# Second mixer of a two-layer trunk: seven block products for half of the values, with weight sums formed earlier and kept in HBM

## The chip, the core and the metric

The kernel runs on one core of a Trainium2 chip. The metric is the device time of one execution in microseconds, as a median over several runs. The engines that matter are TensorE (PE, matmuls), VectorE (DVE), ScalarE (ACT) and GpSimd (POOL). DMA transfers are issued from the queue of SyncE (SP) and, for a few, from POOL's or ACT's queue.

## The reference, cut to what matters

The program is a trunk of two layers over 256 tokens of width 1024. In each layer come an FFN, a mixer and an FFN, each behind an RMS norm and with its result added to the stream. The change bears on the second layer's mixer and on the two FFNs ahead of it (the second FFN of layer 0 and the first of layer 1).

```
def swiglu(x, w_gate, w_up, w_down):
    return (jax.nn.silu(x @ w_gate) * (x @ w_up)) @ w_down
...
def c_mixer(x, w_in, w_out):
    q, k, v = jnp.split(x @ w_in, 3, axis=-1)
    o = moba_attention(to_heads(q, C_HEADS, C_HEAD_DIM),
                       to_heads(k, C_HEADS, C_HEAD_DIM),
                       to_heads(v, C_HEADS, C_HEAD_DIM))
    return from_heads(o) @ w_out
```

With 256 tokens and blocks of 256, the attention of this mixer is plain causal attention with 16 heads of 64. `w_in` is 1024 x 3072: 1024 columns of queries, of keys and of values. The values' first half is the product of the 256 x 1024 normed activations with 512 columns of `w_in`.

## The kernel before, in words

**Matmuls.** Every large product is done in three matmuls (`mm3`, L354 to L356): each operand is cut into a high part (fp32r) and the remainder, and high x high, high x low and low x high are summed in PSUM. An activation of width 1024 lies as 8 tiles of 128 rows, transposed: `xT["h"]` and `xT["l"]` (high part and remainder), with the gain of the norm in them; the norm's factor for a token (`norm["col"]`, `norm["row"]`) is applied after the product.

**Weights.** All weights lie in HBM as chunks of 128 x 2048, in the order in which the program uses them (`weight_chunks`, `_layout`). `Stream` loads a chunk into one of three raw buffers (`raw`, SP's queue), splits it on ACT (`whi`, L231) and DVE (`wlo`, L238) into one of four buffers for split weights, and frees this buffer after the matmuls. A unit is the chunk that one `take` hands out. The split of a unit, in two pieces of 1024 columns most times, is written into the program where an earlier unit is freed (`pump`). Units that come first in a stage keep part of their columns in another place of the buffer (`reset`), and then their pieces are 384, 384 and 1280 wide. A `summed` chunk gets its remainder from a DMA on POOL's queue that adds to what ACT wrote.

**The stages.** The stages are ffn (phase 0), the first mixer (1), ffn (2), ffn (3), the second mixer (4, `c_mixer`) and ffn (5). An FFN takes 22 units for gate and up and 12 for the down projection. In the last FFN, eight of the down projection's blocks are already done by seven products in place of eight. Their weight sums are formed during phases 2 and 3: `begin_sums` loads a chunk (`blocks`), DVE forms sums (L635 to L637), and SP stores them to HBM, at the positions that `AHEAD` lists. The pool for these tiles is the FFN's own.

**The next stage's activations.** `Next` belongs to the stage that follows. During the down projection of an FFN, `Next.pair` adds a finished pair of tiles to the stream, writes high part and remainder (L393 the remainder), and `squares` gathers the sum of squares (L403, L404).

**The second mixer.** Its units come in this order: q0, k0, the values' first half (two units of 4 x 512 columns), q1, k1, q2, k2, the values' second half, q3, k3, and the output projection. Each of the q and k units holds 256 columns, so four heads. `first_tiles` does q0 and k0: it starts with the k tiles that are done, and between them the mean of squares goes to PE (`sums`), POOL takes the root (`rstd`, L362), ACT spreads it over a tile (L473) and PE transposes that (L475, in `spread`). Then come the copies of q (L979 on ACT, L984 on DVE) and of k (L962 on DVE, L998 on ACT, L1000 and L1002 on POOL), four tiles one after another. `token_block` then does half of the values with the activations as the stationary operand: 2 token tiles x 8 tiles of the inner width x 3 matmuls of 512 columns, into two PSUM banks, and `put_v` scales them, writes the high part (L1169 on ACT) and the remainder (L1170 on DVE).

**The heads.** Attention work is slipped between the units. `step()` is called at fixed points of the program, and `Slots` says at which of them a head's scores, its transposition or a weighted sum is written. For one head, `scores` has PE do the product, DVE subtracts the maximum (L1025 adds the mask to one corner, L1040 does the rest in two parts), ACT takes the exponent (L1043) with the sum, DVE the reciprocal (L1046), and POOL scales the probabilities by it (L1050, in two parts of 128 and 256 columns). `turn` has PE transpose the three blocks of a head's probabilities (L1059), and splits them into `pth` and `ptl`. `weighted` multiplies two heads' probabilities with the values. The first four heads have their scores at steps 5 to 8, and their transpositions at steps 9, 9, 11 and 11.

**PSUM.** All eight banks come from one ring of buffers. Which bank an instruction writes, and so whose last reader it must wait for, follows from the order in which they are asked for.

## Time and profile before

| | us |
|---|---|
| median of 3 runs | 924.44 |
| lowest and highest | 923.64 and 924.46 |
| the profiled execution | 924.17 |
| its span in the profile | 922.4 |
| second mixer in it | about 634.4 to 744 |

A row of a timeline has the start in the span, the busy time, the engine and the line, output and inputs, the tile's shape, and how many such instructions follow one another. What stands in brackets is idle time before it and what ended that. PE's records are for pipelined matmuls, so that starts, not busy times, are to be compared. A row of a group has its count, the busy time in all with the mean in ns, and the idle time ahead of it.

### The profile page before, as it was taken

Reading aid. Unit: us, or ns where it says so; the run is one execution under the profiler, and the core shown is the slowest. Engines: PE = TensorE matmul, PEld = TensorE weight load, DVE = VectorE, ACT = ScalarE, POOL = GpSimd, SP = SyncE. Lnnn points to the kernel's source line nnn. Section 1 sums busy time; section 2 is a strip of 40 time slices with the busy share of each in tenths; the row PEclk is TensorE's granted clock in tenths of the full one; section 3 lists DMA queues with packets and bytes.
Section 4 is the critical chain, followed back from the end, with each engine's and each line's share of the span. In section 5 each row is a group of like instructions: output and inputs, shape, how many; then the busy total and the mean of one; then the engine's idle time right before and its main releaser. Section 6 shows DMA issues by size and latency. Waiting matters only on the chain.

```text
span 922.4 us, 18258 instructions
## 1 busy us (share of the span) xinstructions
PE 915.0 (99%) x7583; PEld 896.5 (97%) x7583; DVE 689.8 (75%) x1058; ACT 528.4 (57%) x808; POOL 80.8 (9%) x117
## 2 busy tenths in 40 slices
PE   9999999999999999999999999999999999999997
PEld 9999999999999999999999999999999999999886
DVE  7976556587888867655677666667778799978897
ACT  7754444468667545444564444455776777555574
POOL 0000000033310000000000000001565100000002
PEclk9999999999999999999999999999999999999999
DMA  9765554665256677766556878865533466855681
GB/s 325 272 228 183 180 195 174 228 226 181 93 183 230 220 281 266 296 238 218 187 209 236 305 272 313 318 216 192 184 137 137 119 230 225 277 191 206 223 310 60
DMA packets 33985, 202.15 MB, mean 219 GB/s; under 512 B 3904, under 2 KB 6208, under 8 KB 12528
## 3 DMA queue, kind: packets, MB, share of 16 engines
q1 hardware_dynamic: 32400, 197.79, 59.8%
q0 software_dynamic: 496, 1.77, 0.9%
q10 hardware_dynamic: 1008, 1.44, 0.5%
q8 instruction: 59, 0.97, 0.4%
q14 instruction: 22, 0.18, 0.1%
HBM read 188.14 MB, written 12.85 MB: 218 GB/s over the span
## 4 chain that ended last, share of the span: by engine, by line
PE 93%; issue 4%; DMA 2%; POOL 0%; DVE 0%; ACT 0%; POOLq 0%; DVEq 0%
PE bank L354 30%; PE bank L355 30%; PE bank L356 30%; DMA raw<-in_weights 1%; PE bank L1059 1%; DMA x<-blocks 1%; PE bank L601 1%; DMA xTl<-away 0%; POOL xTl L803 0%; DVE wlo L238 0%; PE bank L604 0%; PE bank L1021 0%; PE bank L1023 0%; PE bank L1022 0%; PE bank L1208 0%
## 5 line engine op out<-in xcount | busy, mean ns | idle before, releaser
L231 ACT ACTIVATE whi<-raw 128x1024 fp32r<-128x1024 f32 (+5 forms) x349 | 331.6, 994 | 280.4 <-issue 154.6
L238 DVE TENSOR_TENSOR wlo<-raw,whi 128x1024 fp32r<-128x1024 f32 (+5 forms) x349 | 390.6, 1149 | 78.8 <-ACT whi L231 77.8
L354 PE MATMUL bank<-xTh,whi 128*128 128x256 f32 x1600 | 442.7, 277 | 0.0
L356 PE MATMUL bank<-xTh,wlo 128*128 128x256 f32 x1600 | 441.8, 276 | 0.0
L355 PE MATMUL bank<-xTl,whi 128*128 128x256 f32 x1600 | 441.8, 276 | 0.0
L355 PEld LDWEIGHTS bank<-xTl,whi 128*128 128x128 f32 x1600 | 300.4, 188 | 0.0
L354 PEld LDWEIGHTS bank<-xTh,whi 128*128 128x128 f32 x1600 | 300.4, 188 | 0.0
L356 PEld LDWEIGHTS bank<-xTh,wlo 128*128 128x128 f32 x1600 | 300.4, 188 | 0.0
L356 PE MATMUL bank<-hTh,wlo 128*128 128x256 f32 x528 | 145.7, 276 | 0.0
L354 PE MATMUL bank<-hTh,whi 128*128 128x256 f32 x528 | 145.7, 276 | 0.0
L355 PE MATMUL bank<-hTl,whi 128*128 128x256 f32 x528 | 145.7, 276 | 0.0
L355 PEld LDWEIGHTS bank<-hTl,whi 128*128 128x128 f32 x528 | 99.1, 188 | 0.0
L354 PEld LDWEIGHTS bank<-hTh,whi 128*128 128x128 f32 x528 | 99.1, 188 | 0.0
L356 PEld LDWEIGHTS bank<-hTh,wlo 128*128 128x128 f32 x528 | 99.1, 188 | 0.0
L687 DVE TENSOR_TENSOR hm<-gs,bank 128x512 f32<-128x512 f32 x44 | 29.9, 683 | 45.4 <-PE bank L356 44.4
L954 POOL MEMSET k<- 64x256 f32 x12 | 3.2, 307 | 565.2 <-ACT whi L231 378.9
L684 DVE TENSOR_TENSOR gs<-bank,row 128x512 f32<-128x512 f32 x44 | 30.1, 686 | 21.3 <-PE bank L356 21.1
L354 PE MATMUL bank<-mixh,whi 128*128 128x256 f32 x128 | 35.7, 279 | 0.0
L356 PE MATMUL bank<-mixh,wlo 128*128 128x256 f32 x128 | 35.4, 277 | 0.0
L355 PE MATMUL bank<-mixl,whi 128*128 128x256 f32 x128 | 35.4, 276 | 0.0
L1050 POOL TENSOR_SCALAR pr<-pr,rl 128x128 f32<-128x128 f32 (+1 forms) x36 | 31.9, 899 | 29.5 <-DVE rl L1046 20.5
L359 ACT ACTIVATE hTh<-hm 128x512 fp32r<-128x512 f32 x44 | 27.1, 619 | 8.8 <-DVE hm L687 8.0
(231 smaller groups left out, 994.1 us busy)
## 6 DMA issues: line engine op xcount, KB each, us to landing
raw<-in_weights SPq DMA_DIRECT2D x139, 1024.0 KB, 5.0
raw<-in_weights SPq DMA_DIRECT2D x12, 768.0 KB, 4.8
blocks<-in_weights SPq DMA_DIRECT2D x9, 1024.0 KB, 10.0
blocks<-blocks SPq DMA_DIRECT2D x9, 1024.0 KB, 8.7
raw<-blocks SPq DMA_DIRECT2D x7, 1024.0 KB, 4.8
raw<-in_weights SPq DMA_DIRECT2D x6, 512.0 KB, 6.6
raw<-in_weights SPq DMA_DIRECT2D x7, 256.0 KB, 5.7
blocks<-block SPq DMA_DIRECT2D x5, 256.0 KB, 8.9
```

Of the source, the lines that this page charges most:

```text
L231: done = nc.scalar.activation(hi, r, AF.Copy)
L238: self.made[u] = done, nc.vector.tensor_sub(lo, r, hi.bitcast(F32))
L354: nc.tensor.matmul(p, sh, mh, start=start, stop=False)
L355: nc.tensor.matmul(p, sh, ml, start=False, stop=False)
L356: return nc.tensor.matmul(p, sl, mh, start=False, stop=stop)
L359: return nc.scalar.activation(hi, src, AF.Copy), nc.vector.tensor_sub(lo, src, hi.bitcast(F32))
L601: nc.tensor.matmul(o, w[0][i][:, cs], xT[m][:, k], start=k == 0 and m == "h" and j % 2 == 0, stop=False)
L684: nc.vector.tensor_mul(g, both(pg), twice(norm["row"]))
L687: nc.vector.tensor_mul(hm, g, both(pu))
L954: nc.gpsimd.memset(pair[j][o, 1].bitcast(F32), 0.0)
L1050: share = engine.tensor_scalar(pr[:, cs], pr[:, cs], rl[:, b : b + 1], None, op0=ALU.mult)
L1059: nc.tensor.transpose(tp[:, i * 128 : (i + 1) * 128], pr[:, i * 128 : (i + 1) * 128], ident)
```

## The change

The values' first half, a product of 2 x 8 tiles of activations with 8 x 2 blocks of 256 columns, is now done by seven block products for each pair of tiles in place of eight. For a pair of inner tiles the activations are four blocks a11, a21, a12, a22 of 128 x 128 and the weights four blocks of 128 x 256. Each of the seven products is three matmuls of 256 columns. The products use the plain blocks, four formed sums of activations and four formed sums of weights.

- **The weights' sums** are formed in phase 2, at positions 5 and 12 of the gate and up units (`FORMED`): `begin_formed` loads one of the two chunks (kind "V"), forms four sums on DVE (new L686 to L689), splits them into high part and remainder on ACT and DVE, and stores these with SP in HBM (new L699), 512 KB each, eight in all.
- **Their way into the mixer.** A V chunk gives two units in place of one. Each takes 768 plain columns out of the raw chunk, split as before in one piece (new L234 and L241), and 1024 formed columns, which two DMAs on POOL's queue bring straight into `whi` and `wlo` (new L246). So the block takes four units, with 21 matmuls of 256 columns each.
- **The activations' sums** of the first six tiles are formed in phase 3's down projection by `Next.form` (new L430 to L434: four combinations and a sum on DVE, then a split of 128 x 512), into tiles of a new pool. Those of the last pair are formed in `first_tiles`, into parts of the mixer's own tiles.
- **The fold.** The seven products lie in four PSUM banks: 1 and 2 share one, 6 has its own, 5 and 7 share one, 3 and 4 share one. ACT copies product 1 out (new L1254), five sums on DVE (new L1259 to L1263) make the two token tiles' values, and `put_v` reads them from SBUF.
- **Other moves.** In this mixer the copies of q0 are written right after its tiles, ahead of the unit of k0. The tiles `pth` and `ptl` come from a pool that is opened after the fold. The pool of `begin_sums` is closed ahead of the down projection.

The diff, cut:

```diff
+FORMED = {(2, 5): 0, (2, 12): 1}
...
+                pieces = [(slice(0, 768), src[:, (step - 3) * 1024 : (step - 3) * 1024 + 768])]
...
+        if step > 2:
+            self.parts[u] = tuple([t[:, i * 256 : (i + 1) * 256] for i in range(7)] for t in (his, los))
+            for to, v in zip((his, los), self.sums[j][step - 3]):
+                nc.gpsimd.dma_start(to[:, 768:1792], v)
+            split(0, raw[:, :768])
...
+        def form(self, i, f, hi, lo):
+
+            a11, a21, a12, a22 = (x1(2 * i + k)[:, t * 128 : (t + 1) * 128] for k in range(2) for t in range(NT))
+            g0, g1 = (self.gain(2 * i + k) for k in range(2))
+            m, s1, s2, s4 = (f[:, j] for j in range(4))
+            nc.vector.tensor_scalar(m, a22, g1, None, op0=ALU.mult)
+            for to, a, g, b, op in ((s1, a21, g0, m, ALU.add), (s2, a11, g0, s1, ALU.subtract),
+                                    (s4, a12, g1, s2, ALU.add)):
+                nc.vector.scalar_tensor_tensor(to, a, g, b, op0=ALU.mult, op1=op)
+            nc.vector.tensor_add(m, m, s2)
+            split(hi, lo, f)
...
+    def begin_formed(gp, i):
...
+            nc.sync.dma_start(t, st.weights[j].rearrange("(p c) -> p c", p=128))
+        yield
...
+        nc.vector.tensor_sub(b11, b12, b11)
+        nc.vector.tensor_sub(b12, b22, b12)
+        nc.vector.tensor_sub(b22, b11, b22)
+        nc.vector.tensor_add(b21, b21, b22)
...
+            split(hi, lo, f)
+            yield
+            with tc.issue_after(st.last.ins):
+                for to, v in zip(st.sums[j][k], (hi, lo)):
+                    nc.sync.dma_start(to, v.bitcast(F32))
+            yield
...
+                        if phase == 3 and c < 3:
+                            nxt.form(c, f, *(s[:, c] for s in nxt.forms))
...
+    def token_sevens(mix, v, p1, step):
...
+        pb = [bank() for _ in range(4)]
+        at = {1: (0, 0), 2: (0, 1), 6: (1, 0), 5: (2, 0), 7: (2, 1), 3: (3, 0), 4: (3, 1)}
...
+            for n, x, q in ((1, plain(0, 0), 0), (2, plain(0, 1), 1), (6, formed(2), 5), (5, formed(1), 3),
+                            (7, formed(0), 6), (3, formed(3), 2), (4, plain(1, 1), 4)):
+                mm3(p[n], *x, w[0][q], w[1][q], i == 0 and at[n][1] == 0, i == KD // 2 - 1 and n in (2, 6, 7, 4))
+            step()
+            st.free()
+        nc.scalar.activation(p1, p[1], AF.Copy)
...
+            nc.vector.tensor_add(u[:, 0], p1, p[6])
+            nc.vector.tensor_add(cv[:, 0], p1, p[2])
+            nc.vector.tensor_add(u[:, 1:], both(pb[2]), twice(u[:, 0]))
+            nc.vector.tensor_add(cv[:, 1:3], u[:, 1:], both(pb[3]))
+            nc.vector.tensor_add(cv[:, 3], u[:, 2], p[5])
+            for t in range(NT):
+                put_v(v, t, cv[:, 2 * t : 2 * t + 2].rearrange("p h c -> p (h c)"))
```

How the order of instructions changes is shown at three places. The first is DVE at the end of the values' block, before. `wlo` is the remainder of a weight piece, `pr` the probabilities of a head, `nm` its maximum, `rl` the reciprocal, `vtl` the remainder of the values.

```order
L1040 ISA pr,nm<-bank,mask,score 128x128
L1040 ISA nm 128x1
L1040 ISA pr,nm<-bank,mask,score 128x256
L1040 ISA nm 128x1
L238 TENSOR_TENSOR wlo<-raw,whi 128x1024
L1046 RECIPROCAL rl<-l 128x2
L238 TENSOR_TENSOR wlo<-raw,whi 128x1024
L1170 SCALAR_TENSOR_TENSOR vtl<-bank,rstd,vth 128x512
L984 TENSOR_TENSOR q<-bank,q 64x256 x2
L1025 TENSOR_TENSOR added<-bank,mask 128x128
```

The same place on DVE now, from the third head's maximum on; `u` and `cv` are the tiles of the fold, `first` is the copy of product 1.

```order
L1104 ISA pr,nm<-bank,mask,score 128x256
L1104 ISA nm 128x1
L1110 RECIPROCAL rl<-l 128x2
L241 TENSOR_TENSOR wlo<-raw,whi 128x1024 x2
L1110 RECIPROCAL rl<-l 128x2
L1259 TENSOR_TENSOR u<-first,bank 128x256
L1260 TENSOR_TENSOR cv<-first,bank 128x256
L1261 TENSOR_TENSOR u<-bank,u 128x512
L1048 TENSOR_TENSOR q<-bank,q 64x256
```

Two 1024-column remainders and the fold's sums now stand between the third head's softmax and the next q remainder; the value remainders come after the fold.

The second place is DVE at the start of the block, first before. The first row of `added` is the first head's mask addition.

```order
L238 TENSOR_TENSOR wlo<-raw,whi 128x1024
L1025 TENSOR_TENSOR added<-bank,mask 128x128
L1040 ISA pr,nm<-bank,added,score 128x128
L1040 ISA nm 128x1
L1040 ISA pr,nm<-bank,mask,score 128x256
L1040 ISA nm 128x1
L238 TENSOR_TENSOR wlo<-raw,whi 128x1024 x2
L1046 RECIPROCAL rl<-l 128x2
L1025 TENSOR_TENSOR added<-bank,mask 128x128
```

And DVE there now:

```order
L241 TENSOR_TENSOR wlo<-raw,whi 128x384 x2
L1089 TENSOR_TENSOR added<-bank,mask 128x128
L1104 ISA pr,nm<-bank,added,score 128x128
L1104 ISA nm 128x1
L241 TENSOR_TENSOR wlo<-raw,whi 128x1280
L1104 ISA pr,nm<-bank,mask,score 128x256
L1104 ISA nm 128x1
L241 TENSOR_TENSOR wlo<-raw,whi 128x1024
L1110 RECIPROCAL rl<-l 128x2
L241 TENSOR_TENSOR wlo<-raw,whi 128x1024
L1089 TENSOR_TENSOR added<-bank,mask 128x128
```

The pieces of q1 (384, 384 and 1280 columns) and of k1 now stand among the first two heads' softmax.

The third place is PE at the transpositions of the third and fourth head, before. `ident` is the identity, `pth` and `ptl` the transposed probabilities, `vth` and `vtl` the values; the rows end with the first weighted sum.

```order
L356 MATMUL bank<-xTh,wlo 128x256
L1059 MATMUL bank<-ident,pr 128x128 x6
L354 MATMUL bank<-pth,vth 128x512
L355 MATMUL bank<-ptl,vth 128x512
L356 MATMUL bank<-pth,vtl 128x512
L354 MATMUL bank<-pth,vth 128x2x128
```

The same two heads on PE now:

```order
L368 MATMUL bank<-xTh,wlo 128x256
L1123 MATMUL bank<-ident,pr 128x128 x4
L366 MATMUL bank<-pth,vth 128x512
L1123 MATMUL bank<-ident,pr 128x128 x2
L367 MATMUL bank<-ptl,vth 128x512
L368 MATMUL bank<-pth,vtl 128x512
L366 MATMUL bank<-pth,vth 128x2x128
```

One matmul of the weighted sum now stands ahead of the last two transpositions of the fourth head. On POOL's queue the loads of the third formed pair stand ahead of the root (`rstd`), those of the fourth behind it and ahead of the copies of k.

More of the change, by code (lines that the diff above doesn't have):

```diff
@@ L724, in ffn @@
                     ahead.pop()()
+                if (phase, n) in FORMED:
+                    forming.append(begin_formed(gp, FORMED[phase, n]))
+                for g in forming:
+                    next(g, None)
                 if n == late - 1:
@@ L749, in ffn @@
             row = norm["half"]
+            for g in forming:
+                assert next(g, None) is None
+            early_stage.close()
             nxt = Next(phase + 1)
+            if phase == 3:
+                forms = tc.tile_pool(name="sp", bufs=1, side="right")
+                sp = forms.__enter__()
+                nxt.forms = [sp.tile([128, KD // 2 - 1, 4, 128], F32R, name=m) for m in ("sxh", "sxl")]
+                f = fp.tile([128, 4, 128], F32, name="sums")
             for c in range(4):
@@ L1128, in first_tiles @@
             st.free()
+            for j in range(2):
+                put_q(j, ps4[j])
         w = st.take()
@@ L1138, in first_tiles @@
         tile_of(ps4[2], w, 0)
+        if then:
+            then()
         step()
@@ L1273, in c_mixer, with formed @@
                 else:
-                    first_tiles(put_q, put_k, step)
-                if c % 2 == 0:
+                    own = [m[:, a : a + 2].rearrange("p k t c -> p (k t) c") for m, a in zip(mix, (6, 2))]
+                    p1 = mp.tile([128, S], F32, name="first")
+                    def formed():
+                        f = wk.tile([128, 2, S], F32, name="sq", bufs=1)
+                        nxt.form(3, f.rearrange("p t (j c) -> p (t j) c", j=2), *own)
+                    first_tiles(put_q, put_k, step, then=formed)
+                    token_sevens(mix, v, p1, step)
+                    late = tc.tile_pool(name="late", bufs=1, side="right")
+                    turned.append(late.__enter__())
+                if c == 2:
                     token_block(lambda t, p: put_v(v, t, p, c * 256), step)
```

69 lines of the change are left out of this document (51 added, 18 removed).

## Prediction

> **What bounds the kernel now.** I read the page first, then the waits of TensorE (PE), then the second mixer as one stretch, and then that stretch engine by engine. The page, and PE's own waits:
>
> ```profile
> span 922.4 us, 18258 instructions
> PE 915.0 (99%) x7583; PEld 896.5 (97%) x7583; DVE 689.8 (75%) x1058; ACT 528.4 (57%) x808; POOL 80.8 (9%) x117
> PE bank L577 <- PEq L1344: 0.8, 1, 0.8
> PE bank L601 <- ACT whi L231: 0.5, 1, 0.5
> 634.00:744.00 110.00, 110.00 (x847) 105.08 (x847) 87.60 (x211) 80.35 (x183) 48.10 (x66) 1.00 0.47 156
> ```
>
> PE waits 1.3 us in all, both times at the start; in the second mixer (last line; PE, weight loads, DVE, ACT, POOL, then granted clock) it has no gap at a clock of 1.00. So time is matmul columns, and any wait that the change brings is lost in full. DVE is busy 87.6 of 110 us there: the engine to watch.
>
> **What the removed matmuls are worth.** Start times on PE: three steps of a 256-column matmul, three of a 512-column one (the second tile of the block), then two groups of transpositions and what follows the first of them.
>
> ```profile
> 640.16 0.28 PE L354 MATMUL bank<-xTh,whi 128*128 128x256 f32 x1
> 640.50 0.28 PE L354 MATMUL bank<-xTh,whi 128*128 128x256 f32 x1
> 650.23 0.39 PE L354 MATMUL bank<-whi,xTh 128*128 128x512 f32 x1
> 650.91 0.39 PE L354 MATMUL bank<-whi,xTh 128*128 128x512 f32 x1
> ...
> 664.08 0.82 PE L1059 MATMUL bank<-ident,pr 128*128 128x128 f32 x6
> 664.66 0.37 PE L354 MATMUL bank<-xTh,whi 128*128 128x256 f32 x1
> 670.20 0.82 PE L1059 MATMUL bank<-ident,pr 128*128 128x128 f32 x6
> ```
>
> A 256-column matmul takes 0.34/3 = 0.1133 us, a 512-column one 0.68/3 = 0.227. Before, the block is 2 x 2 x 4 x 3 = 48 wide ones, 10.90 us; now 4 x 7 x 3 = 84 narrow ones, 9.52 us. **Term 1: -1.38 us.** More there is not to win.
>
> **What the change moves on DVE.** The block used to take two weight buffers for 10.9 us and now takes four for 9.5, with four buffers in the ring. So the units behind it (q1, k1, q2, k2: queries and keys of the next heads) are split only as the short V units let go, beside the softmax of the first heads, and the fold of the seven products comes on top. The rows that time this:
>
> ```profile
> 651.88 1.99 ACT L231 ACTIVATE whi<-raw 128x1024 fp32r<-128x1024 f32 x2
> 615.48 1.58 ACT L231 ACTIVATE whi<-raw 128x768 fp32r<-128x768 f32 x2 [3.43 <-issue]
> 620.96 1.22 DVE L238 TENSOR_TENSOR wlo<-raw,whi 128x1024 fp32r<-128x1024 f32 x1
> 622.09 0.87 DVE L393 SCALAR_TENSOR_TENSOR xTl<-x,gT,xTh 128x256 fp32r<-128x256 f32 x2
> 637.88 0.42 DVE L426 TENSOR_TENSOR acc<-acc,sq 128x256 f32<-128x256 f32 x1
> 641.04 1.03 DVE L238 TENSOR_TENSOR wlo<-raw,whi 128x384 fp32r<-128x384 f32 x2
> 643.25 1.48 DVE L238 TENSOR_TENSOR wlo<-raw,whi 128x1280 fp32r<-128x1280 f32 x1
> 652.14 0.29 DVE L1025 TENSOR_TENSOR added<-bank,mask 128x128 f32<-128x128 f32 x1 [2.00 <-PE bank L1023]
> 653.15 2.99 DVE L238 TENSOR_TENSOR wlo<-raw,whi 128x1024 fp32r<-128x1024 f32 x2
> 658.45 0.17 DVE L1046 RECIPROCAL rl<-l 128x2 f32<-128x2 f32 x1 [0.71 <-ACT pr L1043]
> 658.53 0.33 DVE L1040 CUSTOM_DVE_ANT_0 pr<-bank,mask,score 128x128 f32<-128x128 f32 x1
> L238 DVE TENSOR_TENSOR wlo<-raw,whi 128x1024 fp32r<-128x1024 f32 x6 | 8.1, 1362 | 1.8 <-ACT whi L231 1.7
> ```
>
> Where it starts: ACT began the piece at 651.88, behind the norm's row and the keys. The pieces ahead of that chain are now 768 wide (0.79 us on ACT by the 615.48 row, which makes 1.06 for 1024; 0.3 less on DVE), so I move it up by 0.57, to 651.3; DVE follows 0.5 later, at 651.8. From there DVE's order is fixed, and it has no hole that I can find. Start to start: two 384-column pieces 1.06; one head's softmax 1.01 (652.14 to 653.15); 1280 columns 1.48; six 1024-column pieces (k1, q2, k2); a second softmax 1.01; a third, which needs no mask addition, 1.01 - 0.29 = 0.72; three reciprocals 0.24 (0.08 each, 658.45 to 658.53). That is 5.52 us and the six pieces. A quiet piece takes 1.13 (620.96 to 622.09); in 648 to 665, beside POOL, six took 1.362 us each (last row), 1.28 start to start. 5.52 + 7.68 = 13.20, so the fold's first sum starts at 665.0 and ends at 665.4 (0.42 for 256 columns, by the 637.88 row). I take the 1.28 because its rows are from this very place; the quiet price gives 664.5.
>
> **Term 2, the first wait.** In the built program the second head's transposition goes to the PSUM bank that product 6 leaves, and the last reader of that bank is this first sum. Before, the six transpositions began at 664.08 and took 0.58; now PE is there 1.38 earlier, and at the second head at 664.08 - 1.38 + 0.29 = 663.0. It waits 665.4 - 663.0 = **+2.4 us**; +1.5 with quiet pieces, +4.5 if all six take the 1.66 that the longer of the two at 653.15 took. Behind this wait stand all matmuls; nothing else can run on PE.
>
> **Term 3, the second wait.** It comes one key tile on, at the fourth head. POOL must scale that head's probabilities, and its softmax now lies on DVE behind the fold:
>
> ```profile
> 656.33 0.73 DVE L1170 SCALAR_TENSOR_TENSOR vtl<-bank,rstd,vth 128x512 fp32r<-128x512 f32 x1
> 663.15 0.86 DVE L984 TENSOR_TENSOR q<-bank,q 64x256 fp32r<-64x256 f32 x2
> 666.32 0.17 DVE L1046 RECIPROCAL rl<-l 128x2 f32<-128x2 f32 x1 [1.19 <-ACT pr L1043]
> 656.85 1.52 POOL L1050 TENSOR_SCALAR pr<-pr,rl 128x128 f32<-128x128 f32 x2
> 653.78 1.28 POOL L1000 CAST k<-k 64x256 fp32r<-64x256 f32 x1
> 652.53 0.39 POOL L1000 CAST k<-k 64x256 fp32r<-64x256 f32 x1
> ```
>
> From the fold's first sum DVE has three sums of 256 columns (0.35 each) and two of 512 (0.61; a quarter and a half of the quiet 1.13 and a little for the start), two pairs of query remainders (0.83 each, one cut in two by the fold), the two value remainders (0.66 each), a softmax (1.01) and one piece of transposed probabilities (0.5): 6.6 us, to 671.6. Then a reciprocal 0.1 and POOL, 0.6 for the first part and 0.9 for the second: 672.4 and 673.25. PE, let go at 665.4, needs 0.29, one key unit of 48 x 0.1133 = 5.44 and 0.29 for the third head: 671.4. It waits 1.0, does one transposition and one matmul (0.35), and waits 0.5: about **+1.4 us**. This hardly hangs on term 2, since both ends move with DVE. Before, this head's reciprocal stood at 666.32 and its transposition after 670.20: 3.9 us in hand, which the change uses up.
>
> **What I cost at nothing.** The formed sums come by eight transfers of 512 KB on POOL's queue, ahead of the reciprocal root and the key copies there:
>
> ```profile
> 639.79 0.78 POOL L958 DMA_DIRECT2D mask<-in_consts  x1 [0.97 <-issue]
> 642.42 0.72 POOL L362 TENSOR_TENSOR rstd<-ms,half_neg 128x2 f32<-128x2 f32 x1 [1.84 <-DVE ms L435]
> 643.18 0.70 ACT L473 ACTIVATE wide<-ones,rstd 128x128 f32<-128x128 f32 x2 [0.54 <-POOL rstd L362]
> 645.78 0.27 PE L475 MATMUL bank<-ident,wide 128*128 128x128 f32 x1
> wlo<-in_weights POOLq DMA_DIRECT2D x2, 512.0 KB, 7.8
> blocks<-in_weights SPq DMA_DIRECT2D x9, 1024.0 KB, 10.0
> ```
>
> Two issues (0.78 each) from 640.6 end at 642.2, before the mean is there; the mean itself comes some 0.8 later, behind the early query remainders, and the root's result was 1.9 us early for PE (643.88 to 645.78). Without that cover the delay goes to PE one for one. The last pair is issued by 647.6 and needed at 654.6: 7.8 to land is 0.8 late, 10.0 three late, but then PE meets term 2 that much later, and the sum grows by 0.2 at most. The activations' sums (2.1 us of DVE a time, under down projection tiles of 15 us) and two fewer 1024-column remainders in the mixer lie beside matmuls.
>
> **Sum.** -1.38 + 2.4 + 1.4 = +2.4 us on the profiled execution's 924.17, so 926.6. That run lies 0.27 under the median of 924.44; as a median I forecast **926.8**. With terms 2 and 3 at their ends (1.5 to 4.5, 1.2 to 1.6) this case spans 925.8 to 929.2. About 0.2% (1.85 us) is what a measurement of this kernel can tell from no change: faster is below 922.6, slower above 926.3. Of the forecast's 0.71, 0.20 lies within that band.
>
> **Rivals.** *No wait ends last on PE* (0.13): if DVE gets to the fold's first sum by 663.0, two us earlier than I sum, and to the fourth head by 669, the matmuls' gain stays: 924.44 - 1.4 = 923.0, within 0.2%. For it: today's mixer has no PE gap though ACT and DVE wait on each other often. Against it: the list above has no idle in it, and even quiet pieces are 1.5 late. It decides at a DVE stretch of 10.8 us in place of 13.2.
>
> *The second FFN runs late* (0.07). There DVE already stands still for a block load:
>
> ```profile
> 352.51 2.36 DVE L238 TENSOR_TENSOR wlo<-raw,whi 128x1024 fp32r<-128x1024 f32 x2 [0.27 <-ACT whi L231]
> 359.09 0.69 DVE L635 TENSOR_TENSOR blocks<-blocks 128x512 f32<-128x512 f32 x1 [3.62 <-DMA blocks<-in_weights]
> 363.24 1.22 DVE L238 TENSOR_TENSOR wlo<-raw,whi 128x1024 fp32r<-128x1024 f32 x1
> ```
>
> That split ended at 364.4, not one 5.44 us unit after 354.9, so 4.1 late. A second load beside it (some 3 us), four differences (2.8) and a split (1.2) make 11 late. A piece is normally ready 3.4 us after its buffer is free and used three units, 16.3 us, after: 12.9 of cover. A load 5 us slower than that uses it up by 3 us: 929.8.
>
> *POOL and DVE shut each other out* (0.05). Two pieces at 653.15 took 2.99 in place of 2.26 while POOL's copy took 1.28 in place of 0.39: both lose. If DVE always lost, POOL's work inside the stretch (a key pair 1.1, two heads' scaling 1.5 each) would add 4.1 to the quiet 12.30 (5.52 and six of 1.13), the first wait would be 5.6, and the time 930.0. The Trainium skill (SBUF — State Buffer, "Who interferes with whom") has such a rule: a DVE instruction with two SBUF inputs and a GpSimd one that reads SBUF exclude each other, and whichever started first keeps the port. By that rule, with POOL always first, it would be this 930.0; with DVE always first, 925.9. The trace agrees that they hold each other up, and shows both orders.
>
> Something that I don't see makes it faster by more than the matmuls: 0.04.
>
> **Chances and range.** Slower 0.51 + 0.07 + 0.05 = 0.63, same 0.20 + 0.13 = 0.33, faster 0.04. The range is 923.4 to 929.4: it takes in the forecast's own and reaches towards the first rival, and leaves out that rival's lower half, the other two and what lies beyond.
>
> **What would show it.** Right: PE waits of some 2.4 and 1.4 us at the transpositions of the second and fourth head, the first let go by the fold's first sum on DVE, the second by POOL; DVE unbroken from about 651.8 to 671; 84 matmuls at 0.113. Wrong: PE still without gaps (term 2 wrong), gaps at the formed units (transfers), or gaps in the second FFN.

## The result, and the profile after

The changed kernel takes 930.49 us (median of 6 runs, 929.89 to 931.89) against 924.32 before (6 runs beside them): a ratio of 1.007, interval 1.0057 to 1.0083. It is slower by 6.2 us, where +2.4 had been forecast with a range up to 929.4. The sign and the first two places were right, the size was not. The profiled execution took 930.09; the others that are shown here lie within 2 us of the medians of their kernels.

PE's waits come first. Each row has the waiting tile, who let go, the sum, the count and the longest; the two at the program's start are left out.

```profile
PE bank L1123 <- DVE u L1259: 1.3, 1, 1.3
PE bank L1123 <- POOL pr L1114: 1.1, 1, 1.1
PE bank L1085 <- POOL k L1066: 0.9, 1, 0.9
...
PE bank L1123 <- DVE u L1261: 0.5, 1, 0.5
```

The first two waits are the forecast ones: the second head's transposition, let go by the fold's first sum, and the fourth head's, let go by GpSimd (POOL). The 0.5 belongs to the second head as well. The third wait, for a key copy at the fifth head's scores, was in no list. To see where the time goes, PE's starts are set against the same work before. First after (timeline of PE, with idle time in brackets):

```profile
663.30 0.49 PE L1123 MATMUL bank<-ident,pr 128*128 128x128 f32 x3
665.05 0.30 PE L1123 MATMUL bank<-ident,pr 128*128 128x128 f32 x1 [1.26 <-DVE u L1259]
665.85 0.67 PE L1123 MATMUL bank<-ident,pr 128*128 128x128 f32 x2 [0.50 <-DVE u L1261]
673.32 0.60 PE L1123 MATMUL bank<-ident,pr 128*128 128x128 f32 x4
675.23 0.44 PE L1123 MATMUL bank<-ident,pr 128*128 128x128 f32 x2 [1.07 <-POOL pr L1114]
675.97 0.28 PE L366 MATMUL bank<-pth,vth 128*128 128x256 f32 x1
680.07 0.39 PE L1085 MATMUL bank<-k,q 128*128 128x256 f32 x1 [0.87 <-POOL k L1066]
```

And of the kernel before, the end of the first weighted sum and the fifth head's scores:

```profile
671.55 0.28 PE L354 MATMUL bank<-pth,vth 128*128 128x256 f32 x1
674.63 0.28 PE L1021 MATMUL bank<-k,q 128*128 128x256 f32 x1
```

| place on PE | before | after | after is behind by |
|---|---|---|---|
| transpositions, first and second head | 664.08 | 663.30 | -0.78 |
| third and fourth head | 670.20 | 673.32 | +3.12 |
| narrow part of the first weighted sum | 671.55 | 675.97 | +4.42 |
| scores of the fifth head | 674.63 | 680.07 | +5.44 |
| end of the span | 922.4 | 928.2 | +5.8 |

Nearly all of it is lost between 663 and 680 us. The gain that stands at 663 is 0.8 and not 1.38. Between the first two places PE loses 3.9 us, with waits of only 1.76. Most of the rest is the clock, which the granted clock in the windows shows (the value ahead of the DMA share):

```profile
660.00:665.00 5.00, 3.79 (x34) 3.56 (x32) 5.00 (x13) 4.96 (x13) 3.08 (x3) 1.00 0.95 356
665.00:670.00 5.00, 4.45 (x23) 4.29 (x24) 4.87 (x12) 4.04 (x8) 2.28 (x3) 0.66 0.72 262
```

The matmuls in that stretch step by 0.21 us in place of 0.113:

```profile
666.97 0.41 PE L366 MATMUL bank<-xTh,whi 128*128 128x256 f32 x1
667.18 0.41 PE L367 MATMUL bank<-xTl,whi 128*128 128x256 f32 x1
```

The mean of 0.66 over 5 us is a clock of one half for 3.4 of them, about 1.7 us of matmul time. (What of it reaches the end of the span is a question of its own; the first experiment answers it.) The Trainium skill (TensorE: Matmul & The Clock Gate, "The HAM clock gate (the "warmup" mystery)") names half the clock after an idle window of some 3.4 us; the length agrees with this trace, the condition does not, since PE rested 1.76 us here with transpositions between.

DVE was the engine to watch, and its timeline ran as the sum had it:

```profile
651.89 1.67 DVE L241 TENSOR_TENSOR wlo<-raw,whi 128x384 fp32r<-128x384 f32 x2 [3.40 <-ACT whi L234]
662.15 2.36 DVE L241 TENSOR_TENSOR wlo<-raw,whi 128x1024 fp32r<-128x1024 f32 x2
664.50 0.40 DVE L1259 TENSOR_TENSOR u<-first,bank 128x256 f32<-128x256 f32 x1
671.59 0.15 DVE L1110 RECIPROCAL rl<-l 128x2 f32<-128x2 f32 x1
672.11 2.35 DVE L241 TENSOR_TENSOR wlo<-raw,whi 128x1024 fp32r<-128x1024 f32 x2
```

Forecast were 651.8 for the start, 665.0 for the fold's first sum and 671.6 for the fourth head's reciprocal; measured are 651.89, 664.50 and 671.59. What followed behind that reciprocal was not as forecast. GpSimd's scaling, by shape, is shown in two windows that hold one piece each, the second head's first part and the fourth head's second part:

```profile
L1114 POOL TENSOR_SCALAR pr<-pr,rl 128x128 f32<-128x128 f32 x1 | 2.6, 2567 | 1.9 <-DVE rl L1110 1.9
L1114 POOL TENSOR_SCALAR pr<-pr,rl 128x256 f32<-128x256 f32 x1 | 2.8, 2755 | 0.0
```

Before, the eight parts of the first four heads took:

```profile
L1050 POOL TENSOR_SCALAR pr<-pr,rl 128x256 f32<-128x256 f32 x4 | 4.4, 1106 | 0.0
L1050 POOL TENSOR_SCALAR pr<-pr,rl 128x128 f32<-128x128 f32 x4 | 2.4, 605 | 4.6 <-DVE rl L1046 4.5
```

A part of 128 columns took 2.57 us in place of 0.605, one of 256 took 2.76 in place of 1.11 in the mean. Each lies beside two remainders that DVE does back to back (662.15 and 672.11 in the rows above), and these lost nothing: 2.36 and 2.35 us for two. The Trainium skill (SBUF — State Buffer, "Who interferes with whom") says that a DVE instruction with two SBUF inputs and a GpSimd one that reads SBUF exclude each other, by order of issue. The trace agrees that they do; it adds that GpSimd, once it waits, is passed over by a second DVE instruction that starts later than it.

### The profile page after: what moved, and what is told of

Same layout as the page of the kernel before. It is cut to its first block, busy times and chain, and to the rows that moved or that the text cites. A ratio compares the mean times of both kernels' runs of the same rounds, so it can differ in the third digit from the quotient of the medians.

```text
span 928.2 us, 18435 instructions
## 1 busy us (share of the span) xinstructions
PE 917.1 (99%) x7619; PEld 899.4 (97%) x7619; DVE 709.2 (76%) x1099; ACT 534.0 (58%) x817; POOL 90.5 (10%) x125
## 4 chain that ended last, share of the span: by engine, by line
PE 90%; issue 4%; DVE 2%; DMA 2%; POOL 1%; ACT 0%; POOLq 0%; DVEq 0%; ACTq 0%
PE bank L366 29%; PE bank L367 29%; PE bank L368 29%; DVE wlo L241 1%; PE bank L625 1%; DMA x<-blocks 1%; PE bank L1123 1%; DMA xTl<-away 0%; PE bank L628 0%; POOL xTl L867 0%; POOL pr L1114 0%; DMA x<-in_x 0%; DVE pr L1104 0%; PE bank L1085 0%; PE bank L1310 0%
## 5 line engine op out<-in xcount | busy, mean ns | idle before, releaser
L234 ACT ACTIVATE whi<-raw 128x1024 fp32r<-128x1024 f32 (+5 forms) x349 | 331.4, 991 | 275.2 <-issue 142.1
L241 DVE TENSOR_TENSOR wlo<-raw,whi 128x1024 fp32r<-128x1024 f32 (+5 forms) x349 | 390.2, 1148 | 72.7 <-ACT whi L234 71.7
L1114 POOL TENSOR_SCALAR pr<-pr,rl 128x128 f32<-128x128 f32 (+1 forms) x36 | 38.4, 1080 | 29.3 <-DVE rl L1110 27.3
L246 POOL DMA_DIRECT2D whi<-formed00h x1 | 0.8, 781 | 373.2 <-PE bank L368 373.2
```

What stands on the lines that cost most here:

```text
L234: done = nc.scalar.activation(hi, r, AF.Copy)
L241: self.made[u] = done, nc.vector.tensor_sub(lo, r, hi.bitcast(F32))
L246: nc.gpsimd.dma_start(to[:, 768:1792], v)
L1114: share = engine.tensor_scalar(pr[:, cs], pr[:, cs], rl[:, b : b + 1], None, op0=ALU.mult)
```

## The experiments

**Product 6 copied by ScalarE**, so that DVE's first sum no longer holds the bank:

```diff
-            nc.vector.tensor_add(u[:, 0], p1, p[6])
+            nc.scalar.activation(cv[:, 3], p[6], AF.Copy)
+            nc.vector.tensor_add(u[:, 0], p1, cv[:, 3])
```

> The changed kernel, but ScalarE copies product 6 out of its PSUM bank before the fold's first sum, so that the second head's transposition no longer waits for DVE's sum. Theory A (the bank that the fold holds is the wait): the 1.26 us wait at the second head goes below 0.3, the 3.4 us at half clock behind it go, and the time falls from 930.5 to about 927.5. Theory B (GpSimd's scaling of the second head's probabilities, 2.57 us in place of 0.6 beside DVE's two remainders, ends at the same moment, 664.90): the wait stays at 1.2 and 0.5 us, and the time stays within 0.6 of 930.5.

Measured: 930.25 (ratio to before 1.007, 1.0055 to 1.0085), no change against the 930.49. The wait at the second head is the same, with another name behind it, and the fourth head waits longer (last two rows):

```profile
664.37 0.33 PE L1123 MATMUL bank<-ident,pr 128*128 128x128 f32 x1 [1.27 <-POOL pr L1114]
665.27 0.44 PE L1123 MATMUL bank<-ident,pr 128*128 128x128 f32 x2 [0.57 <-POOL pr L1114]
671.91 0.33 PE L1123 MATMUL bank<-ident,pr 128*128 128x128 f32 x1 [0.40 <-POOL pr L1114]
674.64 0.49 PE L1123 MATMUL bank<-ident,pr 128*128 128x128 f32 x2 [2.16 <-POOL pr L1114]
```

So two things ended the first wait at the same moment, the sum and the scaling, and taking one away was worth nothing. Theory A alone falls.

The run also shows what the half clock at the second head costs. Here the granted clock was 1.00 from 660 to 674 us, behind waits of 1.84, so that PE came to the third head early, at 671.02. Yet nothing was won at the fourth: this run's mixer lies 0.69 us earlier in the span (the transposition in `spread` starts at 645.21, against 645.90 in the changed kernel), and the fourth head's last transpositions start 0.59 earlier (674.64 against 675.23). PE only waited longer, 2.56 us in place of 1.07. Behind that the clock was halved for 3.4 us, and the fifth head's scores, at 680.23, are no earlier than the 680.07 of the changed kernel, which lost time to the key copy instead.

**The first four heads scaled on ScalarE:**

```diff
+                if rows and h < 4:
+                    share = nc.scalar.activation(pr[:, cs], pr[:, cs], AF.Copy, scale=rl[:, b : b + 1])
+                    continue
```

> The changed kernel, but the probabilities of the first four heads are scaled on ScalarE and not on GpSimd. Theory A: the first wait stays at 1.26 us (the fold's first sum), only the 0.5 behind it goes, and the fourth head's 1.07 shrinks: about 929. Theory B (GpSimd, kept from SBUF by DVE, is late at each of the three places): the first wait stays at most 1.2, as the bank is still held, but with the 0.5 the half clock goes, the fourth head's wait of 1.07 goes, and the wait for the key copy (0.87) goes because GpSimd is free: about 926.5.

Measured: 928.96 (1.0051, 1.0035 to 1.0068). Theory A's number is met, but by luck, since neither theory has the mechanism: there are two waits, 1.4 us at the second head (let go by ScalarE's query copy) and 2.2 at the fourth (by ScalarE's scaling). The work left GpSimd and queued on ScalarE.

**The fold ahead of the last release**, so that on DVE it comes before the last two remainders:

```diff
-            step()
-            st.free()
+            if i < KD // 2 - 1:
+                step()
+                st.free()
...
+        step()
+        st.free()
```

> The changed kernel, but the fold is written ahead of the last formed unit's release, so that on DVE its first two sums stand ahead of the third softmax and of the last two 1024-column remainders. Theory A (the fold stands too late on DVE): first sum some 3 us earlier, no wait at the second head but for GpSimd's part (0.5 at most), full clock, fourth head's wait under 0.5: 926 or less. Theory B: the remainders that follow still keep GpSimd from the second head's probabilities, a wait of 0.5 to 1.5 stays there, and the time stays above 928.

Measured: 931.58 (1.0084, 1.0069 to 1.0099). No wait is left at the second head; the fourth waits 2.5 and 1.8 us for GpSimd's scaling, and PE's clock is halved for 6.8 us there. What was put ahead of the second head went to the fourth.

**The formed units' blocks 16 columns further on:**

```diff
-            self.parts[u] = tuple([t[:, i * 256 : (i + 1) * 256] for i in range(7)] for t in (his, los))
+            self.parts[u] = tuple([t[:, SHIFT + i * 256 : SHIFT + (i + 1) * 256] for i in range(7)] for t in (his, los))
...
```

> The changed kernel, but the formed units' blocks lie 16 columns further into the weight buffers, as the other 256-column units do. Theory P (the 0.120 us pace of the 84 matmuls, in place of 0.113, comes from where their operands lie): the pace is 0.113 and PE reaches the second head 0.55 earlier; the time hardly moves (within 0.6 of 930.5), because the wait there grows by as much. Theory Q (the pace is a state of PE that lasts from one pause to the next, or comes from the transfers at 350 to 400 GB/s): the pace stays at 0.119 to 0.120.

Measured: 931.15 (1.0078, 1.0063 to 1.0093). The pace in the block is neither theory's. Nine steps lie between the two rows of each pair, so it is 0.118 at the first pair and 0.113 at the second:

```profile
649.21 0.28 PE L366 MATMUL bank<-whi,sxh 128*128 128x256 f32 x1
650.27 0.28 PE L366 MATMUL bank<-whi,xTh 128*128 128x256 f32 x1
652.00 0.28 PE L366 MATMUL bank<-whi,sxh 128*128 128x256 f32 x1
653.02 0.28 PE L366 MATMUL bank<-whi,xTh 128*128 128x256 f32 x1
```

The 0.113 lasts for 2.4 us of the block. The 0.118 goes on behind the block in the tiles of q1, up to 663, which step by 0.113 in the changed kernel. The 0.120 of the blocks that are not shifted does not appear at all. So the place of the operands is neither shown as its cause nor ruled out.

**The second and fourth head scaled on DVE:**

```diff
-                engine = nc.gpsimd if h < nheads - (4 if rows else 2) else nc.vector
+                engine = nc.gpsimd if h < nheads - (4 if rows else 2) and not (rows and h in (1, 3)) else nc.vector
```

> The changed kernel, but the probabilities of the second and fourth head are scaled on DVE and not on GpSimd. Theory B2 (the delay that stays in the end is set at the fourth head, where GpSimd's second part took 2.75 us in place of 0.92 beside DVE's remainders): the wait there goes, GpSimd is free for the key copies, and the time falls by 2 to 3 us, to about 928. Theory D (DVE's queue is simply full from 652 to 676, whoever scales): the 0.8 us that DVE takes on moves the wait on, and the time stays within 1 us of 930.5.

Measured: 927.71 (1.0042, 1.0027 to 1.0057), 2.8 us less than the change. The waits (all but the one at the start):

```profile
PE bank L1123 <- DVE u L1259: 1.2, 1, 1.2
PE bank L1123 <- DVE pr L1114: 1.1, 1, 1.1
PE bank L367 <- DMA wlo<-formed11l: 0.5, 1, 0.5
PE bank L1085 <- POOL k L1066: 0.2, 1, 0.2
```

Theory B2 holds for the size: without GpSimd's slow pieces the result is near the forecast of 926.8. The clock stayed full in this profile, with waits of 1.2 and 1.1. That the fourth head still waits, now for DVE, speaks for theory D in what is left.

**The transpositions and weighted sums later:**

```diff
-            slots.at((5, 6, 7, 8, 12, 13, 14, 16, 17, 18, 19, 20, 24, 24, 25), scores)
+            slots.at((5, 6, 7, 8, 13, 14, 15, 16, 17, 18, 19, 20, 24, 24, 25), scores)
-            slots.at((9, 9, 11, 11, 16, 16, 19, 19, 21, 21, 23), turn)
+            slots.at((10, 10, 13, 13, 16, 16, 19, 19, 21, 21, 23), turn)
-            slots.at((11, 13, 18, 21), weighted)
+            slots.at((13, 15, 18, 21), weighted)
```

> The changed kernel, but the transpositions of the first two heads come one tile of q or k later, those of the next two and the first two weighted sums two later, and the scores of heads 5 to 7 one later. Nothing is left out. Theory W (the loss is in the waits at these transpositions, DVE and GpSimd catch up behind them): no wait over 0.5 us there, full clock, and the time falls to 923 to 926. Theory D (DVE is short of time through the whole mixer): the waits reappear at the scores and transpositions that follow, and the time stays above 928.

Measured: 928.20 (1.0046, 1.0031 to 1.0061): two waits for GpSimd's scaling (1.6 in sum), one of 1.3 for a key copy, one of 0.3 for a bank of the fold. The waits came back behind the slots that were moved: theory D.

**No fold** (the copy of product 1 and the five sums are left out, and two of the product banks are taken for the values):

```diff
-        nc.scalar.activation(p1, p[1], AF.Copy)
...
-                put_v(v, t, cv[:, 2 * t : 2 * t + 2].rearrange("p h c -> p (h c)"))
+                put_v(v, t, pb[2 * t])
```

> The changed kernel without the fold: the copy of product 1 and the five sums on DVE are left out, and the values are read from two of the four product banks. Theory F (the fold's 2.6 us of DVE are the excess): the waits at the second and fourth head go, and the time is 925 or less. Theory R (the four short units in the ring of four buffers push the remainders of q1, k1, q2 and k2 into the softmax; the fold only adds to it): a wait of 1 us or more remains at the fourth head, and the time stays at 926.5 to 929.

Measured: 926.82 (1.0033, 1.002 to 1.0045), with waits of 1.8 us for GpSimd's scaling at the second head. The fold is worth 3.7 us, more than its 2.6 of DVE time, and even without it the change is slower than before: theory R, at the place of the second head and not of the fourth.

**Pauses in the kernel before**, ten of different length in the FFNs:

```diff
+                for m in times:
+                    e = bank()
+                    for i in range(2):
+                        nc.tensor.matmul(e[:, i * 128 : (i + 1) * 128], ident, ones, start=True, stop=True)
+                    z = fp.tile([128, 256], F32, name="pz", bufs=1)
+                    nc.vector.tensor_copy(z, e[:, :256])
+                    for _ in range(m):
+                        nc.gpsimd.tensor_copy(z, z)
+                    done = nc.tensor.matmul(e[:, 256:384], ident, z[:, :128], start=True, stop=True)
```

> The kernel before with ten pauses put in the gate and up products of the second and third FFN: after a unit, PE does a small matmul, DVE copies it, GpSimd copies the copy 0 to 5 times, and PE may go on only after a matmul on that. Theory G (the clock is halved for 3.4 us when PE rested about half of a 3.4 us stretch): pauses under 1 us leave the clock full, some of 1.5 to 2 us halve it for 3.4 us, those over 2.5 us always; half clock adds about 1.7 us to the pause. Theory H (a pause must itself last over 3.4 us; the drop had another cause): no pause here lowers the clock.

The kernel was executed once, for its trace. The idle times of PE at three of the pauses (brackets):

```profile
354.50 0.49 PE L715 MATMUL bank<-pz,ident 128*128 128x128 f32 x2 [3.49 <-POOL pz L714]
376.06 0.49 PE L715 MATMUL bank<-pz,ident 128*128 128x128 f32 x2 [4.29 <-POOL pz L714]
399.86 0.80 PE L715 MATMUL bank<-pz,ident 128*128 128x128 f32 x2 [4.91 <-POOL pz L714]
```

The windows behind the last two of these, with the granted clock ahead of the DMA share:

```profile
376.80:380.20 3.40, 3.40 (x18) 3.40 (x18) 0.00 (x0) 0.00 (x0) 0.00 (x0) 0.50 1.02 424
397.30:404.00 6.70, 4.14 (x19) 4.15 (x20) 2.84 (x4) 0.63 (x1) 2.38 (x3) 0.50 0.46 120
```

The pause of 3.49 us left the clock full, as a shorter one of 2.15 had; 4.29 halved it for 3.4 us, 4.91 for twice that. So a pause does halve the clock, in steps of 3.4 us, and neither theory has the point at which. G's forecast falls, as 3.49 us were too little. H's forecast that no pause lowers the clock falls too, since some pauses came out longer than 3.49 us; its condition, a rest of over 3.4 us, fails in the mixer, where 1.76 us of rest were enough in the changed kernel. Yet 1.84 us at the same place were not, in the run with product 6 on ScalarE.

**The ring alone**, put into the kernel before: the values' first half in four units of 1024 columns, the same 48 matmuls of 512 columns, no fold, no formed sums.

```diff
+        if step > 2:
+            self.parts[u] = tuple([t[:, i * 512 : (i + 1) * 512] for i in range(2)] for t in (his, los))
+            split(0, raw[:, :1024])
```

> The kernel before, in which the first half of the values alone is changed: its two weight units of 2048 columns become four of 1024. The 48 matmuls of 512 columns, the work of every engine and the transfers stay, with no fold and no formed sums. Theory R (four units in a ring of four buffers push the remainders of q1, k1, q2 and k2 into the softmax of the first heads): waits of 1 us or more at the transpositions, and a time of 925.5 to 928. Theory F (the fold and the new sums are the whole excess): no wait, 924.0 within 0.7.

Measured: 927.16 (1.0035, 1.0022 to 1.0049). PE's waits at the transpositions:

```profile
665.52 0.33 PE L1068 MATMUL bank<-ident,pr 128*128 128x128 f32 x1 [0.85 <-POOL pr L1059]
666.42 0.44 PE L1068 MATMUL bank<-ident,pr 128*128 128x128 f32 x2 [0.57 <-POOL pr L1059]
673.51 0.44 PE L1068 MATMUL bank<-ident,pr 128*128 128x128 f32 x2 [0.75 <-POOL pr L1059]
```

The first piece of q1 on DVE:

```profile
652.52 1.66 DVE L240 TENSOR_TENSOR wlo<-raw,whi 128x384 fp32r<-128x384 f32 x2 [3.41 <-ACT whi L233]
```

GpSimd's scaling of the parts of 128 columns:

```profile
L1059 POOL TENSOR_SCALAR pr<-pr,rl 128x128 f32<-128x128 f32 x4 | 5.2, 1294 | 7.3 <-DVE rl L1055 7.3
```

This is the plainest run of all. Nothing is computed that was not computed before; only the units are shorter, and with them their loads (four of 512 KB in place of two of 1 MB). The first piece of q1's remainder (two of 384 columns) moves from 641.04 to 652.52 on DVE, with DVE idle for 3.41 us ahead of it, and 3.2 us are lost, the waits (2.2 in sum) at the same two places as in the change. GpSimd's parts are as slow as in the changed kernel, 1.29 us in the mean (1.30 there) against 0.605 before. The ring's 3.2 us, the fold's 3.7 and the matmuls' gain of 0.8 add up to 6.1 of the 6.2 us that the change costs, if effects of runs may be added.

**The exponent's table loaded early**, then with the scaling on DVE, then with the early fold as well:

```diff
-            if p == 1 or p == 3 and not rows:
+            if p in (1, 3) and not rows:
...
                         nxt.form(3, f.rearrange("p t (j c) -> p (t j) c", j=2), *own)
+                        nc.scalar.activation(wk.tile([128, 2], F32, name="l")[:, :1], xT["l"][:, 7, :1].bitcast(F32), AF.Exp, scale=0.0)
```

> The changed kernel, but the exponent's table is loaded on ScalarE at the start of the mixer and not after the key copies, right ahead of the split of q1. Theory R: the chain of splits, softmax and fold on DVE begins 1.3 us earlier and so ends earlier; the first wait (1.26) goes, the fourth head's shrinks by the same: 928 to 929.5. Theory D (DVE is full in any case): within 0.7 of 930.5.

> The changed kernel with the early table load and with the second and fourth head's probabilities scaled on DVE. Theory R with GpSimd's share (the waits are the place in time of one chain, and add up): what is left of 1.2 at the second and 1.1 at the fourth head goes by 1.3 each, the time is 925 to 926. If the parts do not add up: 927 to 928, as with the scaling alone.

> As the one before, and the fold written ahead of the last formed unit's release. Theory R: with the table early there is room ahead of the last remainders, no wait at the second head, under 0.5 at the fourth: 924.0 to 925.5; the gain of the matmuls, 0.9 us in the trace, is then the most that can be left, 923.0. Theory S (the sums ahead of the third softmax delay the fourth head as much as they help the second, as in the run with the fold alone put earlier): 926.5 or more.

Measured: 931.47 (1.0082, 1.0069 to 1.0096), 929.57 (1.0056, 1.0041 to 1.0071) and 927.89 (1.0041, 1.0028 to 1.0053). The first two medians lie 1.0 and 1.9 us above those of the same kernels without the early table (930.49 and 927.71); the intervals overlap, so that all that can be said is that nothing was won. In the first, DVE's chain begins at 650.37 and not at 651.89, but the piece of 1280 columns then runs beside GpSimd's key copies and takes 2.03 us, ScalarE stands still from 653.81 to 656.24 for a weight load, and the fold's first sum begins at 664.56, as in the changed kernel (664.50). So an earlier start of the chain does not by itself bring an earlier end. The waits are 1.5 at the second head and 3.5 at the fourth. The third run is as theory S had it.

**The ring with the two heads scaled on DVE, and its control:**

> The kernel before with the values' first half in four units of 1024 columns, as in the run that tried the ring alone (927.2), and the second and fourth head's probabilities scaled on DVE. Theory P (the ring costs time only because GpSimd's scaling then falls beside back-to-back remainders of DVE, 2.55 and 2.75 us a part in place of 0.6 and 0.9): no wait at the transpositions, 924.0 to 925.0. Theory R (DVE's queue is late by itself): waits of 1 us or more stay, now let go by DVE, and the time is 926 or more.

> The kernel before, with only the scaling of the second and fourth head moved from GpSimd to DVE. PE has no gap there, so both theories expect 924.0 within 0.7; it shows whether this move brings anything by itself.

Measured: 925.77 (1.0021, 1.0011 to 1.003) and 924.91 (1.0011, 1.0002 to 1.0021). The control itself costs 0.9 us (0.2 to 1.9), so the ring costs 0.9 over it, with one wait of 0.7 for DVE's scaling at the fourth head and one of 0.2. Of the ring's 3.2 us, GpSimd's slow scaling is thus the larger part, and DVE's own lateness the smaller: theory P in the main.

**Both releasers of the second head gone** (product 6 on ScalarE, two heads scaled on DVE), **then with the third and fourth head one tile later:**

```diff
-            slots.at((9, 9, 11, 11, 16, 16, 19, 19, 21, 21, 23), turn)
+            slots.at((9, 9, 12, 12, 16, 16, 19, 19, 21, 21, 23), turn)
-            slots.at((11, 13, 18, 21), weighted)
+            slots.at((12, 13, 18, 21), weighted)
```

> The changed kernel, with the second and fourth head's probabilities scaled on DVE and product 6 copied out of its bank by ScalarE. Theory A with P (two releasers held the second head, each for itself): with both gone no wait there, the fourth head's 1.1 stays or grows by what the first gave: 926.3 to 927.5. If the first wait is still there, let go by DVE's scaling, DVE's order is the bound and the time is 927.7 or more.

> As the run before, and the transpositions of the third and fourth head and the first weighted sum one tile later, behind the fifth head's scores. Theory P: no wait over 0.3 us but for the last formed load; the time is 923.0 to 924.5, so that the gain of the matmuls is back as far as it goes (0.9). Theory D (the mixer's DVE and GpSimd cannot make up for the moved remainders): a wait comes back at the fifth head's scores, whose key copies are late, and the time is 926 or more.

Measured: 927.88 (1.0042, 1.0027 to 1.0057) and 932.82 (1.0092, 1.0075 to 1.0109). In both, the transposition waits for nothing, and the next matmul that needs a bank of the fold waits in its place; in both a key copy is late as well (0.7 and 4.8). Of the second run, these are the waits, and the key copy on GpSimd:

```profile
PE bank L1085 <- POOL k L1066: 4.8, 1, 4.8
PE bank L366 <- DVE cv L1261: 1.6, 1, 1.6
```

```profile
676.11 2.27 POOL L1064 CAST k<-k 64x256 fp32r<-64x256 f32 x1 [9.57 <-ACT k L1062]
```

The copy took 2.27 in place of the 0.39 of its neighbours, again beside DVE's remainders. That is 1.9 of the 4.8; the rest is DVE, whose step for these keys (L1026) starts only at 675.11, behind two remainders. The lateness of DVE and GpSimd only changes places: theory D.

**Narrow matmuls in the kernel before** (each of the 48 cut in two), **and the early fold with the scaling on DVE:**

```diff
+                    for c in range(2):
+                        cs = slice(c * S, (c + 1) * S)
+                        mm3(pb[t][:, cs], xT["h"][:, kk, ts], xT["l"][:, kk, ts], w[0][k][:, cs], w[1][k][:, cs],
+                            kk == c == 0, kk == KD - 1 and c == 1)
```

> The kernel before, with each of the 48 matmuls of 512 columns in the values' first half cut into two of 256. Theory N (matmuls of 256 columns with the activations as the stationary operand run at 0.120 us, so that term 1 was mis-sized from the start): 96 x 0.120 = 11.5 us in place of 10.9, time 924.6. Theory T (the 0.120 of the changed kernel comes from what runs beside the block there, transfers or the new sums): 96 x 0.1133 = 10.9, time 924.0 within 0.4, pace 0.113 after the first 1.4 us.

> The changed kernel with the fold ahead of the last formed unit's release and the second and fourth head's probabilities scaled on DVE. Theory D (DVE has one queue; what goes ahead of the second head goes behind at the fourth): no wait at the second head, 1.5 to 2.7 us at the fourth, let go by DVE, and 926 to 928. If GpSimd was the cause at the fourth head: 924 to 925.5.

Measured: 924.29 (1.0005, 0.9996 to 1.0015) and 931.30 (1.0079, 1.0066 to 1.0091). The pace in the block, in the narrow kernel:

```profile
653.01 0.28 PE L355 MATMUL bank<-wlo,xTh 128*128 128x256 f32 x1
653.13 0.28 PE L356 MATMUL bank<-whi,xTl 128*128 128x256 f32 x1
```

It is 0.120 with no formed transfer, sum or fold of the change there: theory N, by the pace (the time alone could not tell 924.6 from 924.0). Its blocks lie in the buffers without the 16 columns of shift, as those of the change do, so this run does not rule out their place as the cause either. In the other run no wait is left at the second head, the third waits 0.3, and the fourth waits 4.9 us for DVE's own scaling, far over the 1.5 to 2.7 that theory D gave. DVE's timeline there:

```profile
673.47 0.16 DVE L1110 RECIPROCAL rl<-l 128x2 f32<-128x2 f32 x1
673.54 1.21 DVE L241 TENSOR_TENSOR wlo<-raw,whi 128x1024 fp32r<-128x1024 f32 x1
674.66 0.54 DVE L1114 TENSOR_SCALAR pr<-pr,rl 128x128 f32<-128x128 f32 x2
```

The scaling of 0.54 us stands behind a remainder of 1.21 that nobody waits for yet. No version found beats the kernel before.

## Why the prediction was wrong, point by point

**Term 1 (-1.38 us)** was mis-sized. The 84 matmuls run at 0.120 us and not at the 0.1133 that was read from the projections' weight-stationary matmuls at 640: 48 x 0.227 - 84 x 0.120 = 0.8 us, and PE's lead of 0.78 at 663.30 agrees. The narrow kernel has the same pace in this block without the rest of the change. Its cause is open: with the blocks shifted by 16 columns the pace was 0.118 and 0.113.

**What moves on DVE** was right, to 0.5 us over a chain of 20. That the end of it, the fourth head's reciprocal, was met to 0.01 is luck: the fold's first sum came 0.5 early, and the leg from it to the reciprocal took 7.09 and not 6.6. The ring run shows its cause alone, as the prediction had it: four short units in a ring of four buffers. DVE was busy 16.68 of the 20 us from 652 to 672 before:

```profile
652.00:672.00 20.00, 20.00 (x150) 18.89 (x150) 16.68 (x39) 13.70 (x32) 11.46 (x14) 1.00 0.43 154
```

And after:

```profile
652.00:672.00 20.00, 18.24 (x142) 17.84 (x141) 19.76 (x45) 16.85 (x35) 10.21 (x10) 0.91 0.68 254
```

**Term 2 (+2.4)** was right in place and 0.6 too large (1.26 + 0.50), and incomplete: GpSimd's scaling ended with the sum, and the run that took the sum's hold away gained nothing. DVE's six remainders of 1024 columns took the quiet price, 1.14 from start to start, and not the 1.28 that was chosen; but the two of 384 columns, beside GpSimd's key copies, took 1.67 in place of 1.03. The sum's start at 664.50 lies between the quiet 664.1 and the chosen 665.0.

**Term 3 (+1.4)** is the step that failed. It took 0.6 and 0.9 us for GpSimd's two parts at the fourth head. DVE reached the reciprocal when forecast (671.59 against 671.6), and then the second part took 2.76. The probabilities were ready at 675.2 and not at 673.25, 1.9 us late, and PE went on at 675.23. These 2.0 us, 1.0 at the key copy and 0.4 that comes on behind 680 are the difference between the 5.8 of the profile and the forecast 2.4. The run that scales the second and fourth head on DVE gives 2.8 us back, with the wait of 1.2 at the second head as it was.

**Left out altogether** was the wait of 0.9 for a key copy at the fifth head's scores (1.0 of delay in the table). The two steps of that copy on GpSimd:

```profile
677.87 0.39 POOL L1064 CAST k<-k 64x256 fp32r<-64x256 f32 x1 [2.69 <-ACT k L1062]
678.34 1.67 POOL L1066 TENSOR_TENSOR k<-qk,k 64x256 fp32r<-64x256 f32 x1
```

GpSimd had done the scaling at 675.18 and stood idle for 2.69 us, waiting for ScalarE, whose copy of the keys (677.31) comes behind its copy of the first weighted sum (676.52) and so behind the fourth head. Then the second step took 1.67 us in place of the 0.73 that it takes at its quickest, once more beside two remainders on DVE (from 678.21); with 0.73 it would have been done before PE came.

**The rival that POOL and DVE shut each other out** had the right pair and the wrong loser. It priced DVE as the one that is held up, because a pair of remainders at 653.15 had taken 2.99. What decided was GpSimd, which stood beside quiet remainders. It had 0.05, and its time, 930.0, came near the result by luck, for another reason than it gave. DVE first, its other end, is what the traces show beside these parts of the scaling; but that was priced at 925.9, with nothing for what GpSimd loses.

**The clock** was in no term. Half of it for 3.4 us follows the first wait in this profile. It cost next to nothing, as the fourth head's wait, set by DVE and GpSimd, takes up what PE would win: in the run with product 6 on ScalarE the clock was full up to that head, and its last transpositions start at the same place in the mixer to 0.1 us. One of the six runs of the changed kernel fits this, with a mean clock of 0.999, as before, and a span of 928.2 like that of the profiled run at 0.997.

**The rest:** no gap came from the formed loads in the profiled run (up to 0.6 in others), none from the second FFN, and the root was not late. The costs taken as nothing were nothing in this profile. Three sums of the working are off: the leg behind the fold adds up to 6.76 and not 6.6, term 3's two waits to 1.5 and not 1.4, and the upper end of term 2 to 4.7 and not 4.5. None of them moves the forecast by more than 0.3 us.

## What to carry to other kernels

A shorter unit in a ring of buffers is not the same work in smaller portions: it takes a slot for a shorter time, and what is prepared behind it (here the remainders of the next four units) slides into a busier stretch. Price such a slide with the engines that work beside the busy one, and not with the busy one alone; here GpSimd's instruction took four times as long while DVE's own rows showed nothing. Where several waits stand one behind another on one chain, taking away the first only shows the next, so the sum of the waits is no forecast of what a repair gives.

## What the runs showed of the hardware that was not expected

- GpSimd's scaling of 128 x 128 took 2.57 us in place of 0.605, and a copy of 64 x 256 took 2.27 in place of 0.39, while DVE ran remainders with two inputs back to back at 1.18 each.
- PE's clock was halved for 3.4 us after 1.76 us of rest among transpositions, but not after 1.84 us at the same place in another run, nor after a pause of 3.49 us between projections; 4.29 us there halved it for 3.4 us, 4.91 for 6.8. What is counted is open.
- Matmuls of 256 columns step by 0.113 us in most stretches, and by 0.120 in the values' block of the changed kernel and of the narrow one. A third pace, 0.118, lasted in the run with the pauses from 619 to 705 us, behind a halved clock, and in the changed kernel from 669.3 to 673.3, also behind one, both with a granted clock of 1.00. It seems a state that PE can stay in; what begins and ends it was not found.
